# Two tiles for DSA's index sums, and the index scores of a block emitted ahead of the selection of the block below

## The chip, the cores and the metric

The kernel runs on one core of a Trainium2 chip. The metric is the device time of one launch in microseconds (us), taken as the median over runs. The core has a matrix engine (TensorE, in the rows PE, its weight loads PEld), a vector engine (VectorE, DVE), a scalar engine (ScalarE, ACT), GpSimd (POOL) and a sync engine that issues most DMAs (SyncE, SP). Each engine works through its own list of instructions in order; an instruction that waits holds up all that stand behind it on that engine.

## The reference, cut to what matters

The program is a decoder of two layers over 512 tokens of width 1024. In each layer four groups of heads read the same normed input and run side by side: `hgrn2` (a gated linear recurrence, "hg"), `dsa` (sparse attention with a learned index), `nsa` (compressed, selected and window attention) and `mlstm` ("ml"). Their outputs are joined and projected; a cross attention and a SwiGLU follow. The change lies in dsa's index:

```python
def block(bi):                                     # Q_BLOCK = 128 queries
    rel = jax.nn.relu(jnp.einsum('bthd,bsd->bhts', iqb, ik))      # 8 index heads
    score = jnp.einsum('bhts,bth->bts', rel, iwb).astype(F32)
    causal = key_pos[None, :] <= qpos[:, None]
    score = jnp.where(causal[None], score, -jnp.inf)
    _, idx = lax.top_k(score, topk)                # topk = min(256, l_ // 4) = 128
    ...                                            # attention over the chosen keys
```

## The kernel before, in words

Tokens come in four blocks of 128 (`TB` = 4). The parts of a layer are Python generators; `weave` and `mix` draw from them in turn by an estimated cost, and so fix the order in which instructions are emitted. A list scheduler then orders each engine's list: it takes emitted instructions by priority (earlier emitted first, with exceptions for weights) as its model of the machine says that they become ready. So a late instruction that is ready fills a hole that an early one leaves.

Per layer there are two woven stages. In the first (`run`, the banks `ba`), `dsa` (index and selection, then `hg_space`) is woven with nsa, ml (`ml_in`, `ml`, tiles `m_...`) and the input projections (`ml_in2`, `dsa_in2`, `hg_in`). In the second (banks `bb`), `dsa_attn` and `hg` are woven with `out_stage(0)`, `xa_kv` and `out_stage(1)`.

`dsa` works on blocks 1 to 3 (block 0 needs no choice). `index(tb)` makes the sums `iacc` of block tb over n = (tb+1)*128 keys: PE multiplies one head's queries by the keys into the PSUM tile `dt` (L679, one buffer), ACT takes relu into `rel` (L681), DVE multiplies by the head's weight and adds into `iacc` (L684, L685 for head 0, L688 for the others). `select(tb)` finds the 128th largest: 16 rounds on DVE alone, each a MAX8 (L696) that finds eight maxima and a MATCH_REPLACE8 (L697) that strikes them out of `iacc`; then L700 writes the mask `dmask`. `iacc` has one buffer, so index(tb+1) starts when select(tb) has ended. The tiles `rel` turn in slots with the tag `t2`, four in this pool (`n2=4`), of 512 floats per partition each.

Two further things hang on the end of `dsa`. `hg_space` closes dsa's pool and opens `hgin` in its place, on the right side of SBUF; `hg_in` waits for this before it emits its last two projections, `hgi` and `hgg` (in the rows `acc<-wh,xh`, 256 columns): 8 groups of 24 matmuls, which ACT empties into `h_v` and `h_g` (L485). `acc` has two buffers. And ml's last part, for each block of 128 tokens (a chunk), is a chain: PE makes four score products one after the other into the one-buffered PSUM tile `mb` (L1048), DVE empties each into `m_p` (L1056), PE multiplies with the values (L1065), DVE normalizes (L1069 to L1077, POOL a power at L348) and writes `mo` (in the order rows `mo3`). The output projection (`out_stage(0)`) reads `mo2` and `mo3` through transposes (L1281), and `hg` starts on DVE (L837) behind ml's last `mo3`; at L896 `hg` ends its loop over levels and rewrites `h_k`.

Of the kernel before, what the change touches and what calls it, by code (L numbers as in the profile page):

```python
# [15 lines left out]
D, S, MEM, DEPTH, FF = 1024, 512, 256, 2, 2816  # L16
KC = D // 128
TB = S // 128
# [188 lines left out]
class Kernel:  # L207
# [434 lines left out]
    def dsa(self, pool, keep):  # L642
        nc = self.nc
        idx = self.d_idx
        st = self.t(pool, "d_st", [128, 64], bufs=1)

        ik = idx[:, :, 256:288]
        self.sumsq(st[:, 4:8], ik, pool)
        self.rsqrt(pool, st[:, 8:12], st[:, 4:8], 1.0 / 32, EPS)
        self.tt(ik, ik, st[:, 8:12, None].to_broadcast([128, TB, 32]), OP.mult)  # L650
        self.tt(ik, ik, self.row("idxk_gain")[:, None, :].to_broadcast([128, TB, 32]), OP.mult)
        self.rope(idx[:, :, 256:288].rearrange("p t (h d) -> p t h d", h=1), self.ic, self.isn, 4, pool)
        iq = idx[:, :, 0:256].rearrange("p t (h d) -> p t h d", h=8)
        self.rope(iq, self.ic, self.isn, 4, pool)
        iks = self.t2(pool, "iks", [128, TB, 96], FR)
        nc.vector.tensor_copy(iks[:, :, 0:32], ik)
        nc.vector.tensor_copy(iks[:, :, 32:64], ik)
        self.tt(iks[:, :, 64:96], ik, iks[:, :, 0:32].bitcast(FT), OP.subtract)
        ikT = self.t(pool, "ikT", [128, S], FR, bufs=1)
        self.transpose_blocks(ikT[0:96], lambda j: iks[:, j, :].bitcast(FT), TB, nc.vector.tensor_copy, rows=96,  # L660
                              pool=pool)

        yield 4.0

        def index(tb):
            n = (tb + 1) * 128
            iqs = self.t(pool, "iqs", [128, 8, 96], FR, bufs=1)
            nc.scalar.activation(iqs[:, :, 0:32], iq[:, tb], AF.Copy)
            nc.scalar.activation(iqs[:, :, 64:96], iq[:, tb], AF.Copy)
            self.tt(iqs[:, :, 32:64], iq[:, tb], iqs[:, :, 0:32].bitcast(FT), OP.subtract, nc.gpsimd)  # L670
            iqT = self.t(pool, "iqT", [128, 8, 128], FR, bufs=1)
            for g in range(2):
                self.transpose_blocks(iqT[0:96, 4 * g:4 * g + 4].rearrange("p a b -> p (a b)"),
                                      lambda j: iqs[:, 4 * g + j, :].bitcast(FT), 4, self.act_copy, rows=96,
                                      pool=pool)
            acc = self.t(pool, "iacc", [128, S], bufs=1)[:, :n]
            for h in range(8):
                sc = self.psum("sc", pool=pool)
                nc.tensor.matmul(sc[:, :n], iqT[0:96, h], ikT[0:96, :n], start=True, stop=True)  # L679
                rel = self.t2(pool, "rel", [128, S])  # L680
                nc.scalar.activation(rel[:, :n], sc[:, :n], AF.Relu, scale=1.0 / 16)  # L681
                w = idx[:, tb, 288 + h:289 + h]
                if h == 0:
                    nc.vector.tensor_scalar(acc[:, :n - 128], rel[:, :n - 128], w, None, op0=OP.mult)  # L684
                    nc.vector.scalar_tensor_tensor(acc[:, n - 128:n], rel[:, n - 128:n], w, self.k("neg"),  # L685
                                                   op0=OP.mult, op1=OP.add)
                else:
                    nc.vector.scalar_tensor_tensor(acc, rel[:, :n], w, acc, op0=OP.mult, op1=OP.add)  # L688
                yield 0.7
            return acc  # L690

        def select(tb, acc, masks):
            n = (tb + 1) * 128
            m8 = self.t(pool, "m8", [128, 8])
            for r in range(16):
                nc.vector.max(m8, acc)  # L696
                nc.vector.match_replace(acc, m8, acc, -3e38)  # L697
                yield 0.4 + 0.25 * tb
            masks[tb] = self.t(keep, f"dmask{tb}", [128, n], BF, bufs=1)
            nc.vector.tensor_scalar(masks[tb], acc, -2e38, NEG, op0=OP.is_gt, op1=OP.mult)  # L700

        masks = self.d_masks = {0: None}
        for tb in range(1, TB):
            acc = yield from index(tb)
            yield from select(tb, acc, masks)

    def dsa_attn(self, pool):
        nc, l = self.nc, self.l
# [828 lines left out]
    def run(self):  # L1537
        nc = self.nc
        late = ExitStack()
        for l in range(DEPTH):  # L1540
            self.l = l
            banks = ExitStack()
            self.banks(banks, "ba", tp=1, sc=2, o=1, dt=1, mb=1)
            if l == 0:
                self.load_x(self.i["xT"])
            self.layer_consts()
            if l == 0:
                self.open_sq()
            right, index = ExitStack(), ExitStack()
            self.hqf = self.pool(right, "hgqf", side="right")  # L1550
            self.mo = {2: self.t(self.mp, "mo2", [128, 2, S], bufs=1), 3: self.t(self.mp, "mo3", [128, TB, 256], bufs=1)}
            pd = self.pool(index, "dsa", n2=4, n4=0, side="right")
            self.alias[id(pd)] = {"tp": "dt", "sc": "dt"}
            acc = self.dsa_in(pd)
            if l == 0:
                self.setup()
            self.rstd(row=True)
            if l == 0:
                xd = self.i["xT"]
            else:  # L1560
                xd = self.tc.dram_tile([D, S], FT, name=f"xd{l}")
                for c in range(KC):
                    nc.sync.dma_start(xd[c * 128:c * 128 + 128, :], self.xT[c])
            self.xpool.close()
            late.close()
            late, left = ExitStack(), ExitStack()
            pk = self.pool(late, "keep")
            pn = self.pool(left, "nsa", n2=3, n4=1)
            pm = self.pool(left, "ml", n2=3)
            self.alias[id(pn)] = {}  # L1570
            self.hin = None
            for tb in range(TB):
                with self.first():
                    nc.scalar.activation(self.d_idx[:, tb], acc[tb], AF.Copy, scale=self.rcol[:, tb:tb + 1])
            self.weave((self.chain(self.dsa(pd, pk), self.hg_space(index, right)), COST["dsa"]),
                       (self.chain(self.nsa_in(pn),
                                   self.mix((self.nsa(pn), COST["nsa"]),
                                            (self.chain(self.ml_in(pm),
                                                        self.mix((self.ml(pm), COST["ml"]),
                                                                 (self.chain(self.ml_in2(pm), self.dsa_in2(pk), self.hg_in()), COST["in"]))),  # L1580
                                             COST["mlin"]))),
                        COST["two"]))
            left.close()
            banks.close()
            banks = ExitStack()
            self.banks(banks, "bb", tp=1, sc=1, o=1, dt=1, hb=2)
            self.load_x(xd)
            ph = self.pool(left, "hg", n2=2, n4=0)
            pa = self.pool(left, "dat", n2=3, n4=0)
            px = self.pool(right, "xk", n2=2, n4=1, side="right")  # L1590
            self.alias[id(pa)] = {"tp": "dt"}
            self.attn_done = False
            self.weave((self.dsa_attn(pa), COST["attn"]), (self.hg(ph), COST["hg"]),
                       (self.chain(self.out_stage(0), self.xa_kv(px), self.out_stage(1)), COST["out"]))
            left.close()
            banks.close()
            banks = ExitStack()
            self.banks(banks, "bc", tp=2, sc=2, o=2)
            self.open_sq()
            with ExitStack() as e:  # L1600
                p = self.pool(e, "xa")
                rest = self.xa_in(p)
                right.close()
                self.raws = (self.pool(right, "raw", side="right"), RAWS)
                self.all(self.xa(p, self.pool(e, "xo", side="right"), rest))
            with ExitStack() as e:
                self.ffn(self.pool(e, "ffn"))
            self.raws = (self.wp, 3)
            right.close()
            banks.close()  # L1610
        self.xpool.close()
        late.close()
# [18 lines left out]
```

## Time and profile before

| what | value |
|---|---|
| median of 3 runs | 1665.04 us (1662.25 to 1666.55) |
| the profiled execution | 1668.55 us, of which the span of the profile is 1666.8 |
| PE busy in the span | 1598.7 us (96%) |
| DVE, POOL, ACT busy | 920.8 (55%), 799.8 (48%), 711.5 (43%) |
| mean granted clock of TensorE | 0.978 |

The span falls into two layers. The first woven stage lies at about 50 to 289 us (layer 0) and 880 to 1106 us (layer 1), the second at 289 to 420 and 1106 to 1232 us; cross attention and SwiGLU lie behind each. Matmuls overlap in their pipeline, so a row's mean duration of a matmul is longer than the distance at which the next one starts; the distance is read from start times.

### The profile page before, as it was taken

Reading aid. Unit: us, or ns where it says so; the run is one execution under the profiler, and the core shown is the slowest. Engines: PE = TensorE matmul, PEld = TensorE weight load, DVE = VectorE, ACT = ScalarE, POOL = GpSimd, SP = SyncE. Lnnn points to the kernel's source line nnn. Section 1 sums busy time; section 2 is a strip of 40 time slices with the busy share of each in tenths; the row PEclk is TensorE's granted clock in tenths of the full one; section 3 lists DMA queues with packets and bytes.
Section 4 is the critical chain, followed back from the end, with each engine's and each line's share of the span. In section 5 each row is a group of like instructions: output and inputs, shape, how many; then the busy total and the mean of one; then the engine's idle time right before and its main releaser. Section 6 shows DMA issues by size and latency. Waiting matters only on the chain.

```text
span 1666.8 us, 25488 instructions
## 1 busy us (share of the span) xinstructions
PE 1598.7 (96%) x9262; PEld 1326.0 (80%) x9262; DVE 920.8 (55%) x1760; ACT 711.5 (43%) x1525; POOL 799.8 (48%) x698
## 2 busy tenths in 40 slices
PE   7899997999899989999999999999998999999999
PEld 7878876878788868888898887787877888888887
DVE  5697678976764330344225884779776544124420
ACT  5565453356654443343324443433665433223321
POOL 5664334566448987874412010145662444444442
PEclk9999997999999999999999999979999999999999
DMA  5342212213248999963355733131141233333331
GB/s 162 88 114 79 70 32 86 63 49 107 83 140 290 318 311 315 309 216 90 106 158 180 263 111 133 51 118 52 38 125 33 76 95 91 93 101 95 94 100 66
DMA packets 114365, 212.72 MB, mean 128 GB/s; under 512 B 12984, under 2 KB 30136, under 8 KB 114240
## 3 DMA queue, kind: packets, MB, share of 16 engines
q1 hardware_dynamic: 111888, 206.11, 39.8%
q10 hardware_dynamic: 2032, 3.94, 0.7%
q8 instruction: 73, 1.20, 0.3%
q0 software_dynamic: 320, 1.05, 0.2%
q14 instruction: 52, 0.43, 0.1%
HBM read 170.69 MB, written 40.35 MB: 127 GB/s over the span
## 4 chain that ended last, share of the span: by engine, by line
PE 82%; DVE 9%; issue 2%; DMA 2%; POOL 2%; ACT 2%; SPq 0%; ACTq 0%; POOLq 0%; DVEq 0%
PE acc L329 13%; PE acc L331 13%; PE acc L330 13%; PE sc L330 5%; PE sc L331 5%; PE sc L329 5%; PE acc L339 4%; PE acc L340 3%; PE acc L341 3%; PE hb L856 2%; PE o L574 2%; PE sc L552 2%; PE tp L493 2%; POOL wl L293 1%; PE mb L1048 1%
## 5 line engine op out<-in xcount | busy, mean ns | idle before, releaser
L293 POOL TENSOR_TENSOR wl<-wr,wh 128x512 fp32r<-128x512 f32 (+5 forms) x432 | 548.9, 1279 | 462.0 <-ACT wh L292 441.1
L292 ACT ACTIVATE wh<-wr 128x512 fp32r<-128x512 f32 (+5 forms) x432 | 252.4, 592 | 339.0 <-PE acc L330 137.1
L329 PE MATMUL acc<-xh,wh 128*128 128x512 f32 (+1 forms) x704 | 274.0, 391 | 1.6 <-DVE xT L466 0.7
L330 PE MATMUL acc<-xl,wh 128*128 128x512 f32 (+1 forms) x704 | 272.4, 387 | 0.0
L331 PE MATMUL acc<-xh,wl 128*128 128x512 f32 (+1 forms) x704 | 272.4, 387 | 0.0
L466 DVE TENSOR_TENSOR xT<-acc,xT 128x512 f32<-128x512 f32 (+1 forms) x112 | 67.8, 610 | 215.7 <-PE acc L331 215.5
L329 PEld LDWEIGHTS acc<-xh,wh 128*128 128x128 f32 x704 | 132.7, 189 | 32.5 <-issue 2.4
L331 PEld LDWEIGHTS acc<-xh,wl 128*128 128x128 f32 x704 | 132.5, 188 | 27.6 <-issue 0.4
L330 PEld LDWEIGHTS acc<-xl,wh 128*128 128x128 f32 x704 | 132.7, 189 | 26.4 <-issue 0.2
L329 PE MATMUL acc<-f_gh,wh 128*128 128x512 f32 x352 | 139.0, 397 | 6.7 <-ACT f_gh L1491 6.7
L339 PE MATMUL acc<-wh,xh 128*128 128x256 f32 (+2 forms) x480 | 140.1, 295 | 0.8 <-DMA wh<-whl 0.6
L330 PE MATMUL sc<-xl,wh 128*128 128x512 f32 x352 | 139.7, 397 | 0.0
L330 PE MATMUL acc<-f_gl,wh 128*128 128x512 f32 x352 | 139.3, 397 | 0.0
L331 PE MATMUL acc<-f_gh,wl 128*128 128x512 f32 x352 | 139.3, 397 | 0.0
L331 PE MATMUL sc<-xh,wl 128*128 128x512 f32 x352 | 138.8, 394 | 0.0
L340 PE MATMUL acc<-wl,xh 128*128 128x256 f32 (+2 forms) x480 | 138.4, 290 | 0.0
L329 PE MATMUL sc<-xh,wh 128*128 128x512 f32 x352 | 137.9, 393 | 0.0
L341 PE MATMUL acc<-wh,xl 128*128 128x256 f32 (+2 forms) x480 | 137.2, 288 | 0.0
L318 POOL TENSOR_TENSOR phl<-pr,phl 128x512 fp32r<-128x512 f32 (+3 forms) x72 | 94.7, 1316 | 37.4 <-ACT phl L317 30.9
L317 ACT ACTIVATE phl<-pr 128x512 fp32r<-128x512 f32 (+3 forms) x72 | 44.2, 613 | 137.6 <-DMA pr<-in_wst 127.8
L339 PEld LDWEIGHTS acc<-wh,xh 128*128 128x128 f32 x480 | 92.3, 193 | 5.1 <-issue 1.9
L340 PEld LDWEIGHTS acc<-wl,xh 128*128 128x128 f32 x480 | 92.8, 194 | 1.2 <-issue 0.5
(407 smaller groups left out, 3160.2 us busy)
## 6 DMA issues: line engine op xcount, KB each, us to landing
wr<-in_wst SPq DMA_DIRECT2D x332, 256.0 KB, 2.7
whl<-phl SPq DMA_DIRECT2D x52, 512.0 KB, 3.8
pr<-in_wst SPq DMA_DIRECT2D x52, 256.0 KB, 4.1
wh<-whl SPq DMA_DIRECT2D x52, 256.0 KB, 4.6
wl<-whl SPq DMA_DIRECT2D x52, 256.0 KB, 4.7
wr<-in_wst SPq DMA_DIRECT2D x48, 128.0 KB, 2.6
wr<-in_wst SPq DMA_DIRECT2D x32, 192.0 KB, 2.4
whl<-phl SPq DMA_DIRECT2D x8, 524.0 KB, 3.7
```

The lines of the kernel that those rows point to most:

```text
L292: nc.scalar.activation(hi, raw, AF.Copy)
L293: nc.gpsimd.tensor_tensor(lo, raw, hi.bitcast(FT), op=OP.subtract)
L317: nc.scalar.activation(both[:, 0], raw, AF.Copy)
L318: nc.gpsimd.tensor_tensor(both[:, 1], raw, both[:, 0].bitcast(FT), op=OP.subtract)
L329: self.nc.tensor.matmul(acc, wh, xh, start=(j == 0), stop=False)
L330: self.nc.tensor.matmul(acc, wh, xl, start=False, stop=False)
L331: self.nc.tensor.matmul(acc, wl, xh, start=False, stop=(j == n - 1))
L339: self.nc.tensor.matmul(acc, xh[:, s], wh, start=(first and j == 0), stop=False)
L340: self.nc.tensor.matmul(acc, xh[:, s], wl, start=False, stop=False)
L341: self.nc.tensor.matmul(acc, xl[:, s], wh, start=False, stop=(last and j == n - 1))
L466: self.nc.vector.tensor_add(self.xT[c][:, cols], acc, self.xT[c][:, cols])
L493: self.nc.tensor.transpose(p[:rows, j * 128:j * 128 + 128], src(j), self.ident)
```

## The change

`iacc` gets two buffers, and the slots of `t2` in dsa's pool go from four to three, which keeps the pool's size. `dsa` emits index(1), index(2), select(1), index(3), select(2), select(3) where it emitted index(1), select(1), index(2), select(2), index(3), select(3).

```diff
-            acc = self.t(pool, "iacc", [128, S], bufs=1)[:, :n]
+            acc = self.t(pool, "iacc", [128, S], bufs=2)[:, :n]
...
         masks = self.d_masks = {0: None}
+
+        acc = yield from index(1)
         for tb in range(1, TB):
-            acc = yield from index(tb)
+            after = (yield from index(tb + 1)) if tb < TB - 1 else None
             yield from select(tb, acc, masks)
+            acc = after
...
-            pd = self.pool(index, "dsa", n2=4, n4=0, side="right")
+            pd = self.pool(index, "dsa", n2=3, n4=0, side="right")
```

The scheduler makes other lists of it in both woven stages of each layer; outside of them the lists read the same. Lines behind the edit are three higher in the changed kernel (L1065 becomes L1068). Three places follow, all in layer 0.

DVE before, where the first selection ends: `iacc_587` is block 1's sums, `iacc_1199` block 2's.

```order
L697 MATCH_REPLACE iacc_587<-m8_830,iacc_587 128x256
L351 TENSOR_TENSOR n_bs_1329<-n_blk_1324,n_bs_1329 128x16x32
L700 TENSOR_SCALAR dmask1_1180<-iacc_587 128x256
L473 TENSOR_TENSOR m_x_1256<-acc_1258,R_341 128x512
L684 TENSOR_SCALAR iacc_1199<-rel_1202,d_idx_110 128x256
L685 SCALAR_TENSOR_TENSOR iacc_1199<-rel_1202,d_idx_110,kc_314 128x128
```

Now, at the second round of the first selection: `iacc_847` is block 2's sums.

```order
L696 MAX m8_997<-iacc_587 128x8
L351 TENSOR_TENSOR m_g_1462<-m_w_1465 128x16
L684 TENSOR_SCALAR iacc_847<-rel_850,d_idx_110 128x256
L685 SCALAR_TENSOR_TENSOR iacc_847<-rel_850,d_idx_110,kc_314 128x128
L697 MATCH_REPLACE iacc_587<-m8_997,iacc_587 128x256
L688 SCALAR_TENSOR_TENSOR iacc_847<-rel_856,d_idx_110,iacc_847 128x384
```

The sums of block 2 stand among the rounds of block 1's selection, where they stood behind its mask.

DVE before, at the end of the first woven stage: the last rounds of the third selection (`iacc_2063`) and the normalizing of ml's last chunk (`m_den_3199`).

```order
L1069 COPY m_den_3199<-mb_3188 128x4
L696 MAX m8_2244<-iacc_2063 128x8
L1070 SCALAR_TENSOR_TENSOR m_den_3199<-m_den_3199 128x4
L697 MATCH_REPLACE iacc_2063<-m8_2244,iacc_2063 128x512
L351 TENSOR_TENSOR m_den_3199<-m_den_3199,m_cols_1492 128x4
```

The same chunk now:

```order
L1280 TENSOR_TENSOR xl_3369<-mo2_105,xh_3368 128x512
L1072 COPY m_den_3199<-mb_3188 128x4
L1073 SCALAR_TENSOR_TENSOR m_den_3199<-m_den_3199 128x4
L351 TENSOR_TENSOR m_den_3199<-m_den_3199,m_cols_1490 128x4
L1075 RECIPROCAL m_den_3199<-m_den_3199 128x4
```

No round of a selection is left between them: the third selection's mask stands 63 rows further up than it did (row 320 of DVE's list in place of row 383).

PE before, at the same place: ml's last value products (`mb_3188`), the transposes of its output (`mo3`), and the third of the eight groups of `hgi` and `hgg` (`acc_2970`).

```order
L1065 MATMUL mb_3188<-m_v1_1616,m_p2_3152 128x65
L1065 MATMUL mb_3188<-m_v1_1616,m_p3_3160 128x65
L1281 MATMUL tp_3386<-kc_314,mo3_106 128x128 x4
L339 MATMUL acc_2970<-wh_2879,xh_115 128x256
L340 MATMUL acc_2970<-wl_2880,xh_115 128x256
```

PE now, first at the eighth and last of these groups (`acc_3205`), which stands around the value products of ml's chunk before the last (`mb_2996`):

```order
L339 MATMUL acc_3205<-wh_3080,xh_289 128x256
L340 MATMUL acc_3205<-wl_3081,xh_289 128x256
L1068 MATMUL mb_2996<-m_v1_1651,m_p0_2862 128x65 x2
L1068 MATMUL mb_2996<-m_v1_1651,m_p1_2871 128x65
L1068 MATMUL mb_2996<-m_v1_1651,m_p0_2862 128x65
```

and then behind ml's last chunk:

```order
L1068 MATMUL mb_3188<-m_v1_1651,m_p3_3160 128x65
L329 MATMUL acc_3549<-xh_3350,wh_3552 128x512
L329 MATMUL acc_3721<-xh_3350,wh_3724 128x512
L330 MATMUL acc_3549<-xl_3351,wh_3552 128x512
L331 MATMUL acc_3549<-xh_3350,wl_3553 128x512
```

Six groups of 24 matmuls that stood behind ml's last chunk stand ahead of it, and the first 12 matmuls of the output projection (`acc_3549`, `acc_3721`) stand between that chunk and the transposes of its output.

## Rows read from the trace of the kernel before

**Rows 1.** Windows by stage: start:end, length, engines busy (instructions), PEclk, DMA share, GB/s

```profile
50.00:289.00 239.00, 219.23 (x1447) 182.35 (x1446) 190.69 (x403) 120.38 (x280) 110.12 (x91) 0.93 0.27 76
289.00:420.00 131.00, 128.52 (x935) 104.70 (x934) 102.00 (x206) 66.72 (x167) 79.87 (x85) 1.00 0.25 74
880.00:1106.00 226.00, 215.56 (x1451) 180.19 (x1448) 159.58 (x397) 92.89 (x230) 28.75 (x33) 0.95 0.43 146
1106.00:1232.00 126.00, 125.03 (x946) 104.09 (x947) 98.05 (x203) 61.69 (x158) 78.50 (x84) 1.00 0.23 67
```

**Rows 2.** Windows at the ends of the first woven stage, layers 0 and 1

```profile
236.00:256.00 20.00, 18.12 (x139) 12.77 (x137) 16.70 (x43) 10.98 (x26) 2.29 (x2) 1.00 0.00 1
256.00:279.00 23.00, 15.76 (x64) 13.20 (x65) 20.99 (x53) 4.48 (x11) 4.34 (x10) 0.55 0.37 121
1075.00:1101.00 26.00, 20.38 (x110) 16.75 (x109) 24.59 (x65) 6.94 (x17) 1.39 (x2) 0.67 0.28 94
```

**Rows 3.** Timeline of PE, layer 0: start us, us, what, [idle before <-releaser]

```profile
262.16 0.47 PE L1048 MATMUL mb<-m_hi,m_hi 64*128 64x128 f32 x1 [0.59 <-DVE m_p L1056]
...
263.80 4.53 PE L1065 MATMUL mb<-m_v,m_p 128*128 128x65 f32 x20 [0.73 <-DVE m_p L1056]
272.47 1.09 PE L1281 MATMUL tp<-kc,mo 128*128 128x128 f32 x4 [4.14 <-DVE mo L351]
...
274.05 0.41 PE L339 MATMUL acc<-wh,xh 128*128 128x256 f32 x1
274.26 0.41 PE L340 MATMUL acc<-wl,xh 128*128 128x256 f32 x1
...
278.43 0.28 PE L339 MATMUL acc<-wh,xh 128*128 128x256 f32 x1
278.55 0.28 PE L340 MATMUL acc<-wl,xh 128*128 128x256 f32 x1
```

**Rows 4.** Timeline of ACT, both layers, line L485: the first evacuations into h_v

```profile
272.74 0.82 ACT L485 ACTIVATE h_v<-acc,r 128x256 f32<-128x256 f32 x2
...
1088.70 0.82 ACT L485 ACTIVATE h_v<-acc,r 128x256 f32<-128x256 f32 x2
```

**Rows 5.** DVE groups, layer 0: line, op, count | busy us, mean ns | idle <-releaser

```profile
L696 DVE MAX8 m<-iacc 128x8 f32<-128x512 f32 x16 | 11.1, 692 | 0.2
L697 DVE MATCH_REPLACE8 iacc<-m,iacc 128x512 f32<-128x512 f32 x16 | 10.8, 676 | 0.0
...
L688 DVE SCALAR_TENSOR_TENSOR iacc<-rel,d_idx,iacc 128x384 f32<-128x384 f32 x7 | 8.0, 1147 | 8.3 <-ACT rel L681 8.3
```

**Rows 6.** Timeline of DVE: normalizing of ml's last chunk, both layers

```profile
268.87 0.15 DVE L1069 COPY m_den<-mb 128x4 f32<-128x4 f32 x1
...
275.76 0.42 DVE L351 TENSOR_TENSOR mo<-mo,m_tok 128x256 f32<-128x256 f32 x1
...
1096.78 0.15 DVE L1069 COPY m_den<-mb 128x4 f32<-128x4 f32 x1
...
1102.12 0.42 DVE L351 TENSOR_TENSOR mo<-mo,m_tok 128x256 f32<-128x256 f32 x1
```

**Rows 7.** Timeline of DVE, line L896: the end of hg's loop over levels

```profile
367.64 1.20 DVE L896 TENSOR_TENSOR h_k<-h_k,h_Fk 128x512 f32<-128x512 f32 x1 [1.42 <-POOL h_Fk L351]
...
1182.87 1.57 DVE L896 TENSOR_TENSOR h_k<-h_k,h_Fk 128x512 f32<-128x512 f32 x1
```

**Rows 8.** Windows: early in layer 0, and both stretches from ml's end to L896

```profile
60.00:120.00 60.00, 51.54 (x353) 45.05 (x352) 55.24 (x123) 32.38 (x79) 36.76 (x28) 0.89 0.35 94
276.20:367.60 91.40, 90.62 (x677) 75.58 (x678) 75.44 (x144) 40.25 (x101) 57.56 (x65) 0.99 0.20 57
1102.50:1182.90 80.40, 80.40 (x624) 67.81 (x622) 68.98 (x138) 32.17 (x79) 50.30 (x58) 1.00 0.23 66
```

## The prediction

> **What bounds the kernel now.** I read the windows by stage first. The woven first stage of layer 0 leaves PE idle for 239.0 - 219.2 = 19.8 us and that of layer 1 for 226.0 - 215.6 = 10.4; the second stages only 2.5 and 1.0 [rows 1]. So PE is the bound, and what an edit can win lies in the first stages, as idle PE or as a low clock. Second, I split these stages and found the loss at their ends. In layer 0 PE is idle for 1.9 us between 236 and 256 and for 7.2 between 256 and 279, at a granted clock of 0.55 in the second; in layer 1 it is idle for 5.6 us between 1075 and 1101 at 0.67. DVE is full there, 20.99 of 23 us and 24.59 of 26 [rows 2]. Third, the timeline names the waits: PE stands 0.59 and 0.73 us for DVE between ml's products and 4.14 us for `mo` [rows 3]. DVE is late because the third selection, 16 rounds of 0.692 + 0.676 us, 21.9 us in all [rows 5], runs between these operations. PE has work that would fill the holes, six of the eight groups of `hgi` and `hgg`, but both `acc` buffers are full until ACT empties them into `h_v`, at 272.7 and 1088.7 us [rows 4], and the list has the third group behind ml's last chunk.
>
> The granted clock is 0.55 where PE is idle most, and matmuls of 256 columns start 0.21 us apart there (274.05 to 274.26) and 0.12 apart once it has risen (278.43 to 278.55) [rows 3]: the 1.2 and the 2.4 GHz level.
>
> **What goes: the ends of the first stages.** By the order, the third selection is done before ml's last two chunks, and all eight groups of `hgi` and `hgg` stand ahead of ml's last chunk. Both causes of the idle time are gone. If PE is full there at the high clock, layer 0 gets back 1.9 + 7.2 = 9.1 us of idle time and 15.76 x 0.45 = 7.1 us of slow matmuls; layer 1 gets 5.6 and 20.38 x 0.33 = 6.7 [rows 2]. Together 28.5 us.
>
> **What comes in its place: a bare tail.** The 144 matmuls of six groups, 144 x 0.12 = 17.3 us, no longer stand behind ml's last chunk, where they covered its normalizing. The last chunk's products still go round PE, DVE, PE through one `mb` buffer: three waits of 0.59 and one of 0.73 [rows 3], 2.5 us. Then DVE normalizes for 5.8 us, from 1096.78 to 1102.54 [rows 6], and PE has 12 matmuls of 512 columns for that, each twice 0.12, 2.9 us; 2.9 are left bare. So 5.4 us per layer, 10.8 in both. This is between 0 (other instructions of attention cover it) and 18.2 (the waits cost what the idle time did that stood behind selections in the same windows, 9.1 us per layer); I take 10.8, since its rows are these very operations.
>
> The first weights of the output projection are wanted earlier. POOL is busy for 2.3 of 20 us and the DMA engines move next to nothing between 236 and 256 us [rows 2], so loading and splitting them is hidden; I cost it at nothing. SP's and POOL's lists change only in these stages.
>
> **What is paid in the second stage.** hg starts on DVE behind ml's last `mo`, before and after, and its loop over levels ends at L896. That stretch takes 91.4 us in layer 0 (276.2 to 367.6) and 80.4 in layer 1 [rows 6, 7]. PE is full in it, 90.6 and 80.4 us; DVE has 75.4 and 69.0 [rows 8]. Now the groups that filled PE are gone from it. In layer 0 PE had done some 1.5 us' worth of the 17.3 by 276.2 (2.9 us at the low clock), so 15.8 go and PE is left with 74.8; in layer 1 PE works on them through the 5.8 us of normalizing [rows 6], two thirds of it at the low clock, 4 us' worth, so 13.3 go and 67.1 are left. PE now has less to do there than DVE, and DVE becomes the bound. A stretch in which both want an engine in turn never fills it: from 60 to 120 us DVE has 55.24 of 60 us, 92% [rows 8]. At 92% the stretches take 75.4 / 0.92 = 82.0 and 69.0 / 0.92 = 75.0 us, and PE is idle for 82.0 - 74.8 = 7.2 and 75.0 - 67.1 = 7.9: 15.1 us. The bounds are 0 (PE stays full) and 91.4 - 74.8 + 80.4 - 67.1 = 29.9 (the stretches do not shrink). I take 15.1, from the row of this kernel in which DVE is the busiest.
>
> **Smaller things.** DVE's wait of 8.3 us for `rel` in block 2's sums [rows 5] goes, as the rounds of the first selection stand between them; in the middle of the stage PE is full, so this is worth nothing by itself. In return a `rel` slot is free only when DVE has come past the rounds ahead of its sum, and there are three slots. An ACT instruction that waits for one holds up what is queued behind it on ACT, attention's exponentials and evacuations and the splitting of weights, and PE waits for those. I cost it at nothing, because DVE waits for `rel` now and not the other way; its price is below. The second `iacc` and the fourth slot are equal in size, so nothing else moves in memory.
>
> **Sum.** 28.5 - 10.8 - 15.1 = 2.6 us less. The profiled execution took 1668.55 us, 3.5 more than the median of the three runs, 1665.04; I take the sum off each: 1666.0 for such an execution, and 1662 for the median. A change of 0.3%, 5 us, is about what can be told from none, so this forecast is "no change", on the fast side.
>
> **Rivals.** (a) hg keeps pace, PE finds other work, and the second stage costs nothing: 28.5 - 10.8 = 17.7 less, 1647. For it: the scheduler keeps PE full in the second stages now, 128.5 of 131 us [rows 1]. Against it: DVE would have to be busy for practically all of both stretches.
>
> (b) The slower one: hg's loop is a chain of its own through DVE, POOL, ACT and PE, whose length does not depend on how full PE is. Then the stretches take 91.4 and 80.4 us as before, PE is idle for 29.9 us in them, and the sum is 10.8 + 29.9 - 28.5 = 12.2 more: 1677. For it: L896 itself waits 1.42 us for POOL's `h_Fk` [rows 7], and POOL has 57.6 of the 91.4 us [rows 8]. Against it: between 276.2 and 367.6 PE is idle for only 0.8 us, so PE's list sets the pace there. It decides from the point where L896 comes no less than about 90 us behind ml's last `mo`.
>
> (c) The low clock stays: PE is still idle in pieces in the bare tail and in hg's first levels, at 0.89 as between 60 and 120 us or lower [rows 8], and the 7.1 + 6.7 = 13.8 us of slow matmuls are paid again in a new place: 13.8 - 2.6 = 11.2 more, 1676. For it: the clock fell in both layers where PE waited for DVE in short pieces. Against it: in hg's levels PE would still be busy for 75 of 82 us. The Trainium skill speaks for it ("TensorE: Matmul & The Clock Gate", section "What's actually happening"): the slow clock is the default and only activity lifts it, so an idle hole is paid twice. The 0.55 at the end of layer 0's first stage agrees with that; by this rule alone, the new idle time of 10.8 + 15.1 us would draw the clock down again and (c) would be the outcome.
>
> (d) The wait for `rel` changes sides and stops ACT, and through it PE, in the middle of the first stages. Up to the 8.3 us of layer 0, and as much again in layer 1; at half of that, 8 us, 1662 + 8 = 1670, about the upper edge of no change. For it: DVE has selections in place of idle time there. Against it: PE has projections in stock.
>
> That the selection does not end earlier at all is excluded by the order.
>
> **How the numbers follow.** The forecast has 0.38, (a) 0.24, (b) 0.14, (c) 0.12, (d) 0.12. Around 1662 the forecast's own range is 1655 to 1668, from the middle halves of the two bounds. Faster than 1660: four tenths of the forecast (0.15), nearly all of (a) (0.23) and a little of (d) (0.02), 0.40. Slower than 1670: nearly all of (b) and (c) (0.24) and two fifths of (d) (0.05), 0.29. In between, 0.31. The range reaches from (a) to (b), 1646 to 1677.
>
> **What would show it.** In the changed profile, right: no PE row behind ml's last chunk waits 4 us for `mo`; the windows at the stage's ends have a clock near 1; the first `h_v` comes well before ml's last chunk; the selection's last MAX8 lies some 40 us before the end of the stage. The second term is right if PE is idle for about 5 us around the last transposes of `mo`. The third is right if from ml's last `mo` to L896 (L899 there) there are about 82 and 75 us with DVE near 92%; under 77 and 70 speaks for (a), about 90 and 80 for (b). A granted clock under 0.8 in these windows is (c). ACT rows of `rel` that wait for DVE, with PE idle between 100 and 230 us, are (d). I am wrong altogether if the time moves by more than 5 us and these windows are as forecast.

## The result, and the profile after

The changed kernel takes 1695.7 us (median of four runs, 1691.1 to 1701.2), the kernel before 1665.8 in the same runs: a ratio of 1.0177, 95% interval [1.0158, 1.0196]. It is 30 us slower, where I forecast 2.6 us faster and nothing beyond 1677.

The profiled execution is the shortest of the four, 1691.09 us with a span of 1689.3; its span is 22.5 us longer than that of before. Outside the woven stages nothing moved: what follows them runs 8 us later than before in layer 0 and 22.5 us later in layer 1, from their first projection to the last. So layer 0's woven stages pay 8 us and layer 1's 14.5.

To see where, I cut each layer's woven part into three stretches: early, from there to ml's last `mo`, and from ml's last `mo` to the end of the second stage. The rows of before are new cuts of the trace that [rows 1] cut by stage; the columns are those of [rows 1].

```profile
50.00:150.00 100.00, 90.32 (x627) 77.99 (x626) 80.30 (x163) 60.18 (x145) 63.03 (x48) 0.93 0.35 96
150.00:276.20 126.20, 116.11 (x722) 91.70 (x721) 100.37 (x228) 54.24 (x123) 35.54 (x29) 0.93 0.22 64
276.20:457.10 180.90, 172.53 (x1271) 143.33 (x1270) 139.30 (x278) 95.99 (x236) 106.32 (x112) 0.98 0.26 74
880.00:1010.00 130.00, 125.18 (x915) 109.21 (x913) 94.31 (x249) 54.32 (x141) 15.18 (x15) 0.99 0.54 182
1010.00:1102.50 92.50, 86.88 (x507) 67.48 (x506) 61.80 (x143) 36.53 (x84) 10.79 (x10) 0.91 0.27 93
1102.50:1277.90 175.40, 168.15 (x1252) 140.09 (x1250) 135.81 (x277) 93.39 (x231) 101.96 (x110) 0.98 0.25 73
```

The same stretches after the change, layer 1's first cuts moved by the 8.2 us that it starts later:

```profile
50.00:150.00 100.00, 86.81 (x592) 74.90 (x592) 88.26 (x200) 62.16 (x151) 55.38 (x42) 0.90 0.29 85
150.00:285.60 135.60, 133.93 (x895) 110.64 (x893) 85.51 (x193) 62.85 (x135) 51.05 (x42) 1.00 0.27 76
285.60:465.30 179.70, 163.22 (x1116) 134.09 (x1117) 131.61 (x277) 86.88 (x220) 93.05 (x104) 0.90 0.22 68
888.20:1018.20 130.00, 120.93 (x819) 104.47 (x818) 91.55 (x243) 54.88 (x140) 14.88 (x15) 0.93 0.50 169
1018.20:1128.60 110.40, 109.37 (x728) 90.20 (x727) 64.42 (x151) 43.11 (x100) 18.91 (x17) 0.97 0.32 104
1128.60:1300.50 171.90, 161.57 (x1124) 133.64 (x1124) 132.39 (x274) 85.65 (x219) 92.92 (x103) 0.90 0.21 67
```

What a stretch loses is its idle time, length less PE busy, and what the low clock takes, PE busy times (1 - granted clock). Layer 0's last stretch after the change: 179.7 - 163.22 = 16.5 us idle and 163.22 x 0.10 = 16.3 us of low clock. For both layers together:

| lost, us | early | to ml's last mo | behind it (hg) | sum | profiled time |
|---|---|---|---|---|---|
| before | 22.1 | 31.7 | 22.4 | 76.2 | 1668.6 |
| changed | 39.4 | 6.0 | 59.3 | 104.7 | 1691.1 |

The ends of the first stages are won, 25.7 us; the early stretches lose 17.3 (5.9 in layer 0 and 11.4 in layer 1) and the hg stretches 36.9. That is 28.5 more lost, against 22.5 more span; 6.0 us of it don't close in this reckoning, as the clock is given to two digits and the ends of matmuls are modelled. What the low clock takes is time of PE; how much of it the kernel would get back at the higher clock, the reckoning does not say.

**The ends of the first stages** look as forecast. PE's timeline in layer 0, with the first transposes of `mo` without a wait where 4.14 us stood [rows 3]:

```profile
283.61 0.60 PE L1284 MATMUL tp<-kc,mo 128*128 128x128 f32 x4
...
286.69 0.66 PE L1284 MATMUL tp<-kc,mo 128*128 128x128 f32 x4 [1.06 <-DVE xl L1287]
...
298.17 0.80 PE L329 MATMUL acc<-xh,wh 128*128 128x512 f32 x1 [3.19 <-DVE xT L466]
```

ACT's first evacuations into `h_v`, 41 us earlier than in [rows 4] in layer 0, and in layer 1 15, though that layer starts 8 us later:

```profile
231.88 0.48 ACT L485 ACTIVATE h_v<-acc,r 128x256 f32<-128x256 f32 x1 [0.89 <-PE acc L341]
...
1073.81 0.47 ACT L485 ACTIVATE h_v<-acc,r 128x256 f32<-128x256 f32 x1
```

**The hg stretch of layer 0**, in pieces of 5 us:

```profile
325.00:330.00 5.00, 4.73 (x41) 4.07 (x39) 4.96 (x13) 1.01 (x2) 2.10 (x3) 1.00 0.10 28
330.00:335.00 5.00, 3.37 (x25) 2.74 (x23) 5.00 (x14) 1.77 (x9) 2.53 (x4) 0.89 0.01 3
335.00:340.00 5.00, 4.68 (x19) 3.97 (x19) 4.00 (x10) 1.09 (x5) 1.97 (x4) 0.50 0.00 0
345.00:350.00 5.00, 5.00 (x29) 4.06 (x28) 3.01 (x10) 1.51 (x5) 1.40 (x2) 0.50 0.00 0
355.00:360.00 5.00, 5.00 (x21) 4.22 (x21) 2.86 (x6) 1.16 (x3) 0.23 (x1) 0.50 0.09 30
360.00:365.00 5.00, 5.00 (x36) 3.84 (x35) 2.35 (x4) 1.84 (x5) 1.95 (x3) 0.88 0.08 26
```

PE falls idle for 1.6 us between 330 and 335; then the granted clock is 0.50, the lower level, for 25 us, although PE is busy nearly all the time. (Two of the windows are left out; both have PE busy for 5.00 us at 0.50.) DVE is busy for 2.9 to 4.0 of each of these 5 us. Its operation on hg's products, one row of what its copies waited for, shows who waits for whom:

```profile
  PE hb L859: 8.2, 8
```

So here DVE waits for PE, and the slow PE sets the pace. From ml's last `mo` to L899 these copies wait 8.7 us for PE's products in layer 0, but only 2.1 us in layer 1 (before the change 0.5 and 0.9). PE's timeline shows what ran when the clock was low and when it rose:

```profile
339.02 2.07 PE L859 MATMUL hb<-h_qs,h_ks 64*128 64x128 f32 x8
...
346.14 2.07 PE L859 MATMUL hb<-h_qs,h_ks 64*128 64x128 f32 x8
...
358.38 0.58 PE L339 MATMUL acc<-wh,xm 128*128 128x256 f32 x1
...
363.38 0.28 PE L339 MATMUL acc<-wh,xm 128*128 128x256 f32 x1
```

One head's four products on a level, eight rows, take 2.07 us, again and again, with attention's small matmuls between them. At 358.38 the first projection of `xa_kv` comes, and from 360 to 365 the clock is back (0.88). Layer 1 has the same low clock: PE falls idle for 1.4 us between 1165 and 1170, and the clock is 0.50 from 1170 to 1190. But there it is back before the first projection comes:

```profile
1194.00:1195.00 1.00, 1.00 (x18) 0.88 (x18) 1.00 (x5) 0.50 (x2) 0.00 (x0) 0.97 0.00 0
```

```profile
1195.91 0.39 PE L339 MATMUL acc<-wh,xm 128*128 128x256 f32 x1
```

Only attention's and hg's own matmuls ran ahead of that. So the rows show what preceded the fall, an idle hole in both layers; what brings the clock back they don't show.

The order tells why there was nothing else. Counting projections in units of one 128x256 matmul, and of hg's products in single matmuls, four for each head and level, before the change 150 units stand between hg's 33rd and 81st product in layer 0, and 86 between the 48th and the 96th in layer 1; after it none in either place. (The counts in my expectations below are layer 0's with the products' numbers 16 too high; those that they give for layer 1 are wrong: between the 33rd and the 81st it has 104 before the change, 82 in e6 and 52 in e9.) In the changed kernel the six groups of `hgi` and `hgg` are used up before ml ends, and the output projection behind it by 324 us.

**The early stretch of layer 1** has a hole that was not there. PE's timeline:

```profile
952.11 0.66 PE L574 MATMUL o<-PT,n_tok 128*64 128x128 f32 x8 [0.21 <-ACT PT L497]
955.83 1.09 PE L521 MATMUL tp<-kc,qd 128*128 128x128 f32 x4 [3.07 <-DVE qd L1130]
...
959.92 1.09 PE L493 MATMUL tp<-kc,P 128*128 128x128 f32 x4 [0.88 <-DVE ql L351]
```

and DVE's, which PE waits for:

```profile
953.08 0.27 DVE L700 TENSOR_SCALAR dmask<-iacc 128x256 bf16<-128x256 f32 x1
953.27 0.60 DVE L688 SCALAR_TENSOR_TENSOR iacc<-rel,d_idx,iacc 128x384 f32<-128x384 f32 x1
953.90 1.19 DVE L1183 COPY n_blk<-n_kv 64x496 f32<-64x496 f32 x2
955.12 0.43 DVE L351 TENSOR_TENSOR mo<-mo,spread 128x256 f32<-128x256 f32 x1
955.46 0.22 DVE L1130 COPY qd<-n_qr 128x128 f32<-128x128 f32 x1
```

The end of the first selection (L700), a sum of block 2 (L688) and nsa's block copies (L1183) stand ahead of the `qd` that PE wants. In DVE's list the second of nsa's `n_bs` stood at rows 151 and 153 before; now it stands at 177 and 181, behind block 2's sums and the first selection. Layer 1's trace has the same: the last of these `n_bs` starts at 939.2 us before the change, ahead of the first mask at 944.1, and now at 961.9, behind the mask at 953.1.

### The profile page after: what moved, and what is told of

Its sections match the earlier page's. It is cut to its first block, busy times and chain, and to the rows that moved or that the text cites. A ratio compares the mean times of both kernels' runs of the same rounds, so it can differ in the third digit from the quotient of the medians.

```text
span 1689.3 us, 25474 instructions
## 1 busy us (share of the span) xinstructions
PE 1616.9 (96%) x9258; PEld 1345.9 (80%) x9262; DVE 899.0 (53%) x1760; ACT 713.2 (42%) x1525; POOL 791.7 (47%) x698
## 4 chain that ended last, share of the span: by engine, by line
PE 79%; DVE 8%; POOL 4%; DMA 3%; issue 3%; ACT 2%; SPq 0%; POOLq 0%; ACTq 0%; DVEq 0%
PE acc L329 13%; PE acc L330 13%; PE acc L331 12%; PE sc L330 4%; PE sc L331 4%; PE sc L329 4%; PE acc L339 3%; PE acc L341 3%; PE acc L340 3%; PE hb L859 3%; PE o L574 2%; PE sc L552 2%; POOL wl L293 2%; PE tp L493 2%; DMA pr<-in_wst 2%
```

## The experiments

After the result I held three theories. A: hg's levels lose their clock because no projections lie between their products. B: hg's levels are a chain through DVE, POOL and ACT with a length of its own (my rival (b)). C: the loss is DVE's crowding early in the first stages. Each run was timed with the kernel before in the same set. The losses of all of them, reckoned as above, are those of the one execution that was profiled. For e2 it is the slowest of four (1718.7 us), for e9 and e10 the fastest of nine and of twelve (1669.5 and 1658.7), so their losses do not stand for the medians beside them:

| lost, us | early | to ml's last mo | hg | sum | median, us | ratio to before, 95% |
|---|---|---|---|---|---|---|
| e1, six groups held back | 41.7 | 26.7 | 34.9 | 103.3 | 1689.2 | 1.0139 [1.0124, 1.0154] |
| e2, block 2 alone ahead | 36.5 | 28.7 | 70.4 | 135.6 | 1712.1 | 1.0271 [1.0234, 1.0308] |
| e3, additional matmuls | 36.3 | 6.2 | 37.3 | 79.8 | 1692.1 | 1.0163 [1.0146, 1.0180] |
| e4, three slots only | 19.9 | 29.7 | 23.0 | 72.6 | 1664.9 | 0.9993 [0.9984, 1.0003] |
| e5, block 3 alone ahead | 23.9 | 13.2 | 69.4 | 106.5 | 1689.8 | 1.0134 [1.0111, 1.0156] |
| e6, half held | 38.2 | 15.3 | 23.6 | 77.1 | 1669.6 | 1.0022 [1.0008, 1.0036] |
| e7, e5 and e6 together | 22.2 | 21.0 | 28.0 | 71.2 | 1659.9 | 0.9965 [0.9953, 0.9977] |
| e8, e5 with DSA's share 60 | 27.0 | 25.0 | 31.4 | 83.4 | 1672.4 | 1.0037 [1.0025, 1.0050] |
| e9, short selection | 22.6 | 4.4 | 49.5 | 76.5 | 1681.0 | 1.0093 [1.0067, 1.0118] |
| e10, four and two held | 19.5 | 22.2 | 29.8 | 71.5 | 1661.3 | 0.9982 [0.9970, 0.9993] |
| e11, two and four held | 18.9 | 23.6 | 28.5 | 71.0 | 1663.9 | 0.9993 [0.9981, 1.0005] |

**e1: the groups back beside hg.** What I call ml's chunks, above and in the expectations, are its four heads: the chain of score products, values and normalizing runs once for each head, over all four blocks of 128 tokens. `ml_done` is set behind the fourth. In `proj_tok`, for the last two groups of `hgi` and all of `hgg`:

```diff
+            if hold is not None and tb >= hold:
+                while not self.ml_done:
+                    yield 0.5
+                self.act_copy(acc[0:1, 0:1], self.mo[3][0:1, 0, 192:193])
             self.mm_tok(acc[:, :n], w, x, tb)
```

> The changed kernel, but six of the eight groups of hgi and hgg (144 matmuls of 256 columns per layer) wait for ml's last chunk by one 1x1 copy each, so that they lie beside hg's levels again. Theory A (hg's levels lose their clock because no projections lie between their products any more: 13.5 us of low clock between 325 and 363 us in layer 0, 13.4 between 1165 and 1195 in layer 1): the 26.9 us come back, 1695.7 - 26.9 = about 1669, within 1660 to 1675, and the granted clock beside the levels is near 1. Theory B (hg's levels are a chain through DVE, POOL and ACT that sets its own length): the stretch stays as long, and the groups that wait leave holes in the first stage: 1690 to 1700. Theory C (the loss is DVE's crowding early in the first stages, the holes at 112 to 120 and 952 to 960 us): they stay as they are, 1690 to 1697.

1689.2 us: theory A's time was missed by 20 us, and yet the hg stretches did as A has it. The hg stretches lose 34.9 in place of 59.3, 24.4 of the 26.9 us expected. But the ends of the first stages lose 26.7 in place of 6.0. The window of [rows 2] from 256 to 279 us:

```profile
256.00:279.00 23.00, 16.24 (x89) 13.30 (x88) 10.26 (x31) 6.14 (x16) 3.90 (x10) 0.68 0.33 109
```

PE has 16.24 us there at 0.68, before the change 15.76 at 0.55, but DVE is busy for 10.3 us where it had 21.0. The selection is long gone, and PE stands nearly as idle as with it: without the selection, but with the groups late, the ends lose 26.7 us in place of 31.7. The projections are one stock, and ml's last chunk and hg's levels both live on it.

**e2: only block 2's sums ahead.**

```diff
-        for tb in range(1, TB):
-            after = (yield from index(tb + 1)) if tb < TB - 1 else None
-            yield from select(tb, acc, masks)
-            acc = after
+        after = yield from index(2)
+        yield from select(1, acc, masks)
+        yield from select(2, after, masks)
+        acc = yield from index(3)
+        yield from select(3, acc, masks)
```

> Only block 2's sums are emitted ahead of block 1's selection; block 3's sums stand behind block 2's selection again. By the order no projection lies between hg's 48th and 96th product, as in the changed kernel. Theory A: the clock falls beside hg's levels again, 1685 to 1700. Theory B: hg starts where the first stage ends, so the time lies between the two kernels, about 1680. Theory C: the crowding of DVE is less, as one pair of sums and selections is apart again: 1668 to 1678.

1712.1 us, outside every expectation; in the profiled execution, 6.6 us slower than the median, 70.4 us are lost behind ml, 49.2 of them by the low clock. The ends are as poor as before (28.7) although the six groups run before ml ends. The window ahead of the selection's end, ACT's first evacuation into `h_v`, and DVE's last operation of the selection:

```profile
245.00:262.00 17.00, 12.36 (x71) 8.41 (x69) 16.86 (x34) 5.83 (x13) 5.10 (x4) 0.75 0.20 61
```

```profile
262.92 0.84 ACT L485 ACTIVATE h_v<-acc,r 128x256 f32<-128x256 f32 x2 [2.94 <-DVE dmask L700]
```

```profile
261.95 0.94 DVE L700 TENSOR_SCALAR dmask<-iacc 128x512 bf16<-128x512 f32 x1
```

Here `h_v` waits 2.94 us for the third mask itself: the groups can't be emptied until the selection has ended, so they never lie beside it. The selection's hole from 245 to 262 us stays, and nothing is left for hg.

**e3: additional matmuls between hg's products.** Two matmuls of 512 columns ahead of each head's products on levels 1 to 4, into the bank that the products then overwrite:

```diff
                 sc = self.psum("hb")
+                for j in range(more):
+                    nc.tensor.matmul(sc, self.ks0[0][:, 0:128], self.ks0[0], start=True, stop=True)
...
+                for head, sc, regions in products(pr, kk, qs[pr], h, 2 if 1 <= lvl <= 4 else 0):
```

> The changed kernel with 32 additional matmuls of 512 columns per layer, two ahead of each product of hg's levels 1 to 4, into the bank that the product then overwrites: pure extra work for PE, 64 x 0.235 = 15 us at the high clock. Theory A: the clock stays up in the levels, 26.9 us come back and 15 are paid: 1680 to 1690, faster than the changed kernel although it does more. Theory B: the levels' chain through the other engines is as long as before and PE has more to do: 1696 to 1711. Theory C: the same as B.

1692.1 us, between what A and what B gave. The interval overlaps the changed kernel's, so "faster" is not shown; but 64 more matmuls cost no time. The hg stretches' clock went from 0.90 in both layers to

```profile
284.60:460.10 175.50, 163.53 (x1150) 131.27 (x1149) 133.52 (x277) 87.40 (x220) 92.44 (x104) 0.96 0.24 69
1122.50:1299.90 177.40, 165.27 (x1162) 133.58 (x1160) 135.65 (x275) 88.30 (x221) 92.06 (x104) 0.96 0.22 67
```

and the timeline of PE has such eight rows at the same place in little more than half the time:

```profile
338.81 0.71 PE L857 MATMUL hb<-xh 128*128 128x512 f32 x2
339.45 1.16 PE L861 MATMUL hb<-h_qs,h_ks 64*128 64x128 f32 x8
```

Two of the added matmuls take 0.64 us to the start of the products (338.81 to 339.45), about 20 us for all 64, more than the 15 reckoned. The low clock takes 13.2 us of the hg stretches in place of 32.5: the higher clock made the room for the added work.

This alone does not decide between A and B, for the levels did not get shorter: from ml's last `mo` to their end layer 0 takes 84.5 us in place of 85.5, and layer 1, where more of attention and of `xa_kv` now stands among hg's products, 84.3 in place of 75.7. The traces of all kernels say more. The stretch from hg's 33rd to its 97th product, levels 1 to 4, takes in the changed kernel (both layers), in e3 (layer 0) and in e7 below (both layers):

```profile
324.07:366.49 42.42, 40.20 (x223) 33.45 (x223) 30.12 (x73) 12.01 (x36) 15.52 (x21) 0.68 0.05 15
1156.04:1194.83 38.79, 37.41 (x202) 31.57 (x201) 32.03 (x73) 9.92 (x30) 15.67 (x20) 0.65 0.05 17
```

```profile
323.03:362.93 39.90, 39.90 (x266) 30.62 (x265) 31.76 (x75) 14.84 (x45) 17.96 (x23) 1.00 0.09 28
```

```profile
314.82:354.24 39.42, 39.20 (x288) 31.94 (x287) 36.55 (x79) 16.57 (x45) 21.06 (x25) 1.00 0.16 45
1132.69:1171.80 39.11, 39.11 (x288) 31.99 (x287) 35.85 (x79) 16.33 (x45) 21.34 (x26) 1.00 0.17 48
```

The same cut of every trace gives a clock of 0.54 to 0.68 in the stretches that lost their projections (both layers of the changed kernel, e2 and e5, layer 0 of e9; in layer 1, 28 units are left ahead of the 49th product), and 1.00 in all others, which kept projections there or have the added matmuls. That is A's first half: the levels lose their clock where the projections are gone. The second half, that they get longer by it, is not shown. The changed kernel's products take 42.4 and 38.8 us, e7's 39.4 and 39.1, with 65 and 86 matmul rows more. The low clock costs what PE could have done beside the products. Whether bare products would be faster at the higher clock no run tells, and so a length of their own (B) stays open: no trace has this cut under 36.5 us.

**e4: three slots, nothing else.** In the kernel before:

```diff
-            pd = self.pool(index, "dsa", n2=4, n4=0, side="right")
+            pd = self.pool(index, "dsa", n2=3, n4=0, side="right")
```

> The kernel before with three rel slots in place of four and nothing else (PE's, ACT's, POOL's and SP's lists are the same as before). Theories A, B and C: 1665, within 3 us. If the missing slot is what costs (my rival (d), a wait for rel that stops ACT): 1670 to 1695.

1664.9 us, no difference. In the order of before, the slots on which my rival (d) rested cost nothing; for the order of the change the trace answers (below).

**e5: only block 3's sums ahead.** The loop of the change becomes

```diff
+        yield from select(1, acc, masks)
+        acc = yield from index(2)
+        after = yield from index(3)
+        yield from select(2, acc, masks)
+        yield from select(3, after, masks)
```

> Only block 3's sums are emitted ahead of block 2's selection; block 1's selection stands directly behind its own sums, as before the change. DVE's list has nsa's block copies (n_bs) at rows 151 and 153 again, as before, and not at 177 and 181; PE's list again has no projection between hg's 48th and 96th product. Theory C (the early hole comes from the first selection and block 2's sums standing together ahead of nsa's block copies): the hole of layer 1 (5.8 us idle and 5.9 of low clock between 948 and 1008 us, before the change 1.6 and 0) is gone, 10 us less than the changed kernel, about 1686. Without C: 1696. Theory A: the low clock beside hg's levels stays, about 13 us in each layer, in either case.

1689.8 us. The early stretches lose 23.9 us, before the change 22.1, with both sums ahead 39.4; layer 1's hole is gone:

```profile
883.00:1013.00 130.00, 125.83 (x888) 109.54 (x887) 93.97 (x250) 54.91 (x143) 16.57 (x16) 0.97 0.54 184
1114.90:1300.30 185.40, 176.77 (x1124) 145.83 (x1123) 133.33 (x274) 86.09 (x217) 92.76 (x103) 0.82 0.19 57
```

C holds, for 15.5 us of the early stretches. The time falls by 5.9 us only: the ends of the first stages lose 7.2 us more than in the changed kernel and the hg stretches 10.1 more, as the second row, layer 1's hg stretch, has a clock of 0.82 in place of 0.90. The kernels that have block 2's sums ahead (changed, e1, e2, e3, e6) lose 36.3 to 41.7 us early, the others 18.9 to 27.0.

**e6: half held.** As e1, but three of the six groups wait only for ml's third head:

```diff
+                while self.ml_heads < (4 if tb >= late else 3):
+                    yield 0.5
+                self.act_copy(acc[0:1, 0:1], self.mo[3][0:1, 0, (192 if tb >= late else 128):(193 if tb >= late else 129)])
```

> The changed kernel with six groups of hgi and hgg held, but three of them only until ml's third head is done and three until its fourth: half of the cover beside ml's last chunk, half beside hg's levels (between hg's 48th and 96th product 96 and 108 units of 256 columns, before the change 150 and 144, changed kernel 0). Theory A: the clock beside hg's levels stays near 1 and ml's end is half covered, idle time and low clock of the second stages go from 60 us in the changed kernel to about 30 and those of the first stages from 45 to about 52: 1695.7 - 23 = about 1673. If the projections are only pushed from one hole into the other, as in the run with all six held: 1685 to 1692.

1669.6 us, 26 less than the changed kernel: the hg stretches lose 23.6 and the ends 15.3. Half of the cover does most of the work in each place, where all of it in one place starves the other.

**e7: both.** e5's loop and e6's hold, with nothing else; the call for the gates is then

```diff
+        yield from self.proj_tok("hgg", lambda tb: self.h_g[:, tb], 256, self.x, hold=0, late=1)
```

> Both of the last two edits: block 3's sums alone ahead, and half of the groups held. If A and C hold and add up: 1695.7 - 23 - 10 = about 1663, as fast as the kernel before or a little faster. If the two losses are not apart: 1673 or more.

1659.9 us: the two losses are apart and add up. It beats the kernel before by 0.35% [0.23, 0.47]. No run divides the groups in the kernel before, so what moving block 3's sums is worth by itself is not shown. Layer 1's early and hg stretches:

```profile
876.00:1006.00 130.00, 126.59 (x899) 110.21 (x897) 95.46 (x251) 55.94 (x145) 16.58 (x16) 0.99 0.56 189
...
1097.50:1271.00 173.50, 165.31 (x1211) 138.09 (x1211) 139.83 (x276) 93.00 (x234) 99.27 (x107) 0.96 0.23 65
```

**e8: by weights alone.** e5's loop, and a smaller share for DSA, so that an order near that of before comes about without any hold:

```diff
-COST = {"dsa": 74.0, ...
+COST = {"dsa": 60.0, ...
```

> Block 3's sums alone ahead, and DSA's share in the weaving 60 in place of 74, so that its steps are emitted later; nothing is held by copies. By the order the projections lie between hg's products as before the change (from the 32nd to the 112th 48, 48, 40, 34, 36 units; before 34, 56, 60, 34, 36). Theory A and C: no low clock beside hg's levels, no early hole, ml's end as before: 1658 to 1668. If emitting sums ahead costs by itself: 1675 or more.

1672.4 us, a miss, between the two expectations. Each of the three columns loses some us more than in e7 (27.0, 25.0, 31.4), though the projections stand between hg's products much as before. Which instruction costs it I did not follow up.

**e9: less selection, nothing reordered.** In the kernel before:

```diff
+                a = acc[:, :64] if tb == 3 else acc
+                nc.vector.max(m8, a)
+                nc.vector.match_replace(a, m8, a, -3e38)
```

> The kernel before, with nothing moved by hand, but block 3's selection looks at 64 of its 512 columns only (what it selects is therefore wrong; 16 rounds stay, each much shorter): some 20 us less work for DVE in each layer, ahead of the ends of the first stages. By the order the scheduler then puts the groups of hgi and hgg ahead of ml's last chunk by itself, and in layer 0 no projection is left between hg's 48th and 96th product. My first term (the ends of the first stages are slow because the selection runs between ml's operations): 1666 - 28 = about 1638, at most 1650. Theory A (PE's projections are one stock that covers either ml's end or hg's levels): layer 0 loses about 13 us of low clock and some idle time beside hg's levels and gains at its end, layer 1 has 32 units there, half covered: 1660 to 1685, no faster than before although DVE has 40 us less to do.

1681.0 us (1669.5 to 1693.3): the third selections take DVE 13.9 us in place of 43.7 in both layers, 30 us less (I had reckoned 40), and the kernel is 0.9% slower. The scheduler moves the groups forward by itself; the end of layer 0's first stage is clean, and its hg stretch pays:

```profile
150.00:281.70 131.70, 129.43 (x868) 105.49 (x866) 89.48 (x230) 63.13 (x140) 45.32 (x37) 1.00 0.23 71
281.70:459.80 178.10, 168.26 (x1120) 139.27 (x1120) 136.13 (x275) 86.80 (x219) 93.70 (x104) 0.87 0.23 67
```

In this execution the sum of losses is that of before (76.5 and 76.2 us), only moved: 27.3 us won at the ends, 27.1 paid behind ml. This is the change's effect without the change: what lets the groups go early takes them from hg. The median is 11.5 us above this execution, and the granted clock of the whole falls with it, from 0.974 in the fastest of the nine runs to 0.961 in the slowest; where the slower ones lose it no trace shows.

**e10 and e11: other shares.** In e7's call for the gates `late=2` (four groups held to the third head and two to the fourth) and `late=0` (two and four):

```diff
-        yield from self.proj_tok("hgg", lambda tb: self.h_g[:, tb], 256, self.x, hold=0, late=1)
+        yield from self.proj_tok("hgg", lambda tb: self.h_g[:, tb], 256, self.x, hold=0, late=2)
```

> The version with block 3's sums alone ahead and half of the groups held, but four of the six held until ml's third head is done and two until its fourth, in place of three and three. Theory A: the total moves little, since both holes are partly covered either way: 1656 to 1664.

> The same with two groups held until ml's third head is done and four until its fourth. Theory A: ml's end has less cover and hg's levels more: 1656 to 1666, the side of the three-and-three version on which it falls says which hole is the dearer.

1661.3 and 1663.9 us. Neither is better than three and three. The table's sums are the same within 0.5 us, so the trace doesn't say why e11's interval lies above e7's.

## Why the prediction was wrong

- **What goes at the ends: right, 25.7 us of 28.5.** That both causes had to go was right too: with the selection gone and the groups late (e1) the ends lose 26.7, with the groups early and the selection late (e2) 28.7, with both mended 6.0. What I did not draw from this is that the cover was spent there.
- **The moved sums, costed at nothing: the step with the largest miss, 17.3 us.** I took the early part as worth nothing and looked for a price in `rel` slots alone (rival (d)). The slots cost nothing in the order of before (e4), and in the changed kernel ACT's rows of `rel` wait for PE alone:

```profile
  PE dt L679: 49.7, 27
```

  What block 2's sums did was to push nsa's block copies behind the first selection in DVE's list, 26 rows on, and PE waited for what stood behind; without them ahead 15.5 us come back (e5). The rows were in the order of both kernels; I compared them at the ends only.
- **The bare tail and the second stage: wrong in mechanism, and by 11.0 us.** I costed them at 10.8 + 15.1 us, all as idle time, with PE at the high clock and DVE at 92% as the bound. Together with the rest of the hg stretches they cost 36.9. The bare tail is 5.0 us of it, in place of 10.8: around the last transposes of `mo` PE is idle for 3.6 us in layer 0 (276 to 295 us) and 1.4 in layer 1 (1118 to 1143). (The 5.8 us of normalizing that I took from [rows 6] held a round of the third selection and its mask besides; without them it takes 4.7 and 6.0.) The lengths from ml's last `mo` to L899 came out near, 85.5 and 75.7 us, forecast 82 and 75, and so did PE's idle time in them, 11.7 us, forecast 15.1. That was luck: DVE is busy for 76% and 82% of them, not 92%, and PE is not short of work but slow, at a clock of 0.80 and 0.82:

```profile
285.60:371.10 85.50, 77.04 (x483) 62.17 (x483) 64.74 (x137) 25.68 (x66) 39.47 (x51) 0.80 0.13 41
1128.60:1204.30 75.70, 72.51 (x473) 59.54 (x472) 62.15 (x133) 23.79 (x61) 39.19 (x50) 0.82 0.15 51
```

  Over the whole hg stretches the idle time rises by 11.2 us (15.6 to 26.8) and the low clock takes 25.7 us more than before (6.8 to 32.5). DVE is not the bound; in layer 0 its waits for PE show that PE is, and in layer 1 PE works for 20 us without a gap at 0.50. That the levels alone would have been shorter at the high clock is not shown; what is shown is that with the projections back PE does more in the same time (e3, e7).
- **Rival (c) is what happened behind ml, and I gave it 0.12.** I priced it at the 13.8 us that the ends had paid before; it came to 25.7. The sign that I had set for it, a clock under 0.8, was just missed (0.80 and 0.82). I spoke against it with a busy share: 75 of 82 us. Busy says nothing here: PE is busy for 5.00 of 5 us in window after window at 0.50. The Trainium skill's rule ("TensorE: Matmul & The Clock Gate", section "What's actually happening"), that the slow clock is the default and activity lifts it, pointed to (c). The trace agrees in that the clock fell behind an idle hole, of 1.6 us in layer 0 and 1.4 in layer 1, but not in that a PE that counts as busy has it back: for 25 us it had not.
- **Rivals (a) and (b).** (a) needed a PE that stays full at the high clock. (b) had the stretches at 91.4 and 80.4 us with PE idle for 29.9 us in them; they took 85.5 and 75.7 with 11.7, so it did not come as priced. That the levels have a shortest length of their own is not excluded (e3).

Between the two failed steps and the sum: -25.7 at the ends, +17.3 early, +36.9 behind ml, against a forecast of -28.5, 0 and +25.9. The misses are 2.8, 17.3 and 11.0 us; less the 6.0 that don't close, they make the 25.1 us between the forecast's 2.6 less and the 22.5 more of the profiled span.

## What to carry to other kernels

Work that fills PE beside a slow chain is a stock: count in the order, before and after, how much of it stands beside each place that needs it, and ask what an earlier stage that now runs smoothly has taken from a later one. Compare the order along the whole of a stage that the edit touches, and not only where the gain is expected. Where a stretch loses its large matmuls, price it at the lower clock too, as the dear case, even if PE would count as busy there. A gain can be kept by dividing the cover: here half for each hole turned 1.8% slower into 0.2% slower (e6), and 0.35% faster with block 2's sums left where they were (e7).

## What the hardware showed

TensorE stayed at the lower level for 25 us while the profile counts it as busy for nearly all of them. With 32 more matmuls per layer, whose results were thrown away, the hg stretches had 0.96 in place of 0.90, and the kernel took no more time (1692.1 us, changed 1695.7). Eight rows of hg's products took 2.07 us at the lower level and 1.16 at the higher. The runs of e9, with 22 us of low clock in layer 0's hg stretch of the fastest, lie within 23.8 us of each other (nine runs), those of e7 within 5.2 (eight).
